# First half of a hybrid attention layer: gate weights split on ACT and DVE instead of POOL, meta columns copied on POOL, squares of x moved into stick-breaking, the first gate pair's weights made ahead

## The chip, the cores and the metric

The kernel runs on 1 core of one Trainium2 chip. Its metric is the time of one execution on the device in microseconds (us), the median of several runs. A core has five engines that run on their own and wait for each other by semaphores: PE (matrix products into PSUM), DVE (vector), ACT (scalar and activation), POOL (general) and SP, which here issues every DMA from one queue in order.

## The reference

One decoder layer, float32, on 2048 tokens of width 1024 with 16 meta tokens ahead of them. All projections come from one matrix `w_in`:

```python
xn = rms_norm(h, norm_gain[l])
proj = xn @ w_in[l]
sb_q, sb_k, sb_v, sw_q, sw_k, sw_v, sb_z, sw_z, g_sb, g_sw = jnp.split(proj, offsets, axis=-1)
o_sb = stick_breaking_attention(sb_q, sb_k, sb_v, valid)          # 8 heads of 64, all earlier keys
o_sw = sliding_window_sink_attention(rope(sw_q), rope(sw_k), sw_v, attn_sinks, valid)   # 16 heads, window 128
y_sb = (o_sb * jax.nn.silu(sb_z)) @ w_branch_sb[l]
y_sw = (o_sw * jax.nn.silu(sw_z)) @ w_branch_swa[l]
merged = jax.nn.sigmoid(g_sb) * y_sb + jax.nn.sigmoid(g_sw) * y_sw
h = h + merged @ w_out[l]
return rms_norm(h, final_norm_gain)[:, BLOCK:]
```

In stick-breaking attention the weight of a key is its sigmoid times the product of (1 - sigmoid) over the keys between it and the query, so it is a running product along the row of scores.

## The kernel before, in words

**Precision.** Every float32 operand is held as two tiles, h (rounded to what PE multiplies) and l (the remainder), and a product is three matmuls: h by h, h by l, l by h. For weights `split` makes the two from a loaded `raw` tile of 128 x 1024. Two switches say where: `hsplit` puts h on ACT (L109) or on POOL (L111), `vsplit` puts l on DVE or on POOL (both L112). Results are evacuated the same way (`evac_split`, L115 on ACT and L116 on DVE). `weights` loads, splits and stores the two halves in DRAM (`kept`), so that the second half of the sequence only loads them.

**Halves and stages.** The sequence (stored in reverse) is worked in two halves of two groups, a group being 512 tokens; a gate or projection tile is 128 columns of `w_in` times a group: 24 matmuls (L415 to L417). Each half has three stages: sliding window (its projections, with that attention between them), stick-breaking, and pairs. Then come the last two gate tiles and the normalised x of the next half, and after both halves the closing stage (`finish`: branch projections, merge, output projection, norm).

**Stick-breaking** (`stick`): 8 heads by 2 groups are 16 units (h, g). A unit's first row loads its keys, values and queries (`load_kv`, `load_q`: kt, vc, q). A row is scores on PE (L1038), a sigmoid on ACT (L1041), a running product on DVE (the scans L1048 and L1050). Where the row ends at the oldest keys, its last 16 columns, the meta tokens, are copied to a small tile (L1054, ACT). Five steps later the row is transposed (L1063), split by ACT and DVE, and multiplied with the values (L1094); meta columns go through `turn_meta` (L1073). `weave` puts these steps between the gate tiles' matmuls: `gts[1]` and `gts[2]` run alone first, `gts[3]` to `gts[REST - 1]` woven in (REST is 12 in the first half, 18 in the second).

**Pairs**: two gates over two groups are a 2 x 2 block product, done in seven products of 12 matmuls each (L685, `seven`) instead of eight. Its x operands, sums of group tiles, are made once on DVE and ACT (`sums_of_x`, L601 to L627); its weight operands t1, t3, t2, t4 by `pair_weights` from two raw tiles a and b (h on ACT, L647; l on DVE, L648; the sums s and s4, L653 to L658). The first three take wh and wl tiles, of which there are three each, shared with all other weights. The first half has six pairs; for the first three of them (`plain`) the two columns' own weights are stored for the second half, for the others the pair's operands. Each result is evacuated through L700 to L715 and gated (sigmoid on ACT, L724; products on DVE, L726 and L730; o is loaded into the ring of four tiles xs, `ring_x`).

**Squares.** The second half's RMS norm needs sums of squares of 1024 tokens: 16 tiles of x, each loaded into the same ring and squared with an accumulator on ACT (L1367), four per pair during the first four pairs.

**Order.** PE's instructions run in the order of the program. DVE, ACT, POOL and SP are ordered by a planner that simulates the kernel when it is built, so an instruction may be moved ahead of others on its engine; on the chip each engine then runs its list in order. Tiles of a name rotate: `tmp` has 7, xs 4, raw 2, wh and wl 3 each; a new use waits until the old one has been read.

Of the kernel before, what the change touches and what calls it, by code (L numbers as in the profile page):

```python
# [47 lines left out]
def tile_kernel(ctx, tc, x, xt, meta, metat, gain, w_in, w_sb, w_sw, w_out, sinks, fgain,  # L48
# [104 lines left out]
    def drain(*gens):  # L153
        for _ in chain(*gens):
            pass
# [194 lines left out]
    def sums():  # L350
        return tp.tile([P, 2, 4], F32, tag="ssq", name="ssq", bufs=3)
# [278 lines left out]

    def pair_weights(bp, ca, cb, plain):

        t1, t3, t2 = ([wp.tile([P, KT, P], F32R, tag=t, name=t, bufs=3) for t in ("wh", "wl")] for _ in range(3))
        t4 = [bp.tile([P, KT // 2, P], F32R, tag=t, name=t, bufs=2) for t in ("s4h", "s4l")]
        key = w_in.name, ca, cb
# [4 lines left out]
        else:  # L640
# [19 lines left out]
            if plain:  # L660
                for c in (ca, cb):
                    kept[w_in.name, c] = [dram(f"{e}_{w_in.name}_{c}", [P, KT, P], F32R) for e in "hl"]
                for k, t in zip(kept[w_in.name, ca], t1):
                    DMA(k, t)
                for k, t, u in zip(kept[w_in.name, cb], t5, t2):
                    DMA(k[:, lo], t)
                    DMA(k[:, hi], u[:, hi])
            else:
                kept[key] = []
                for n, ts in enumerate((t1, t3, t2, t4)):  # L670
                    kept[key].append([dram(f"p{n}{e}_{ca}", list(t.shape), F32R) for e, t in zip("hl", ts)])
                    for k, t in zip(kept[key][n], ts):
                        DMA(k, t)
# [292 lines left out]

    def stick(groups, bp):
        kt, vc = {}, {}
        rows_of = {}
        mask = []  # L970
        bp.tile([P, 4, P], F32R, tag="v", name="vc", bufs=5)
# [46 lines left out]
        def row(h, g, n, j):  # L1018

            if n == j == 0:  # L1020
                load_kv(h, g)
                state[h, g] = {"q": load_q(h, g), "last": {}}
            st = state[h, g]
            last = st["last"]
# [28 lines left out]
            if end:  # L1053
                A.copy(pair(h, g)[0][:, j, h % 2], r[:, w - NM:w])  # L1054

# [238 lines left out]
    for half, groups in enumerate(halves):  # L1294
# [42 lines left out]
        with tc.tile_pool(name=f"sb{half}", bufs=1, side="left") as bp:  # L1337
            vsplit[0] = False
            side = stick(groups, bp)
            drain(tiles_by_tile(gts[1:3], groups))  # L1340
            rest = REST[half]
            cost_sb = 8 * sum(4 * (4 - g) for g in groups) * 1.31 + 8 * 0.75
            ratio = cost_sb / ((rest - 3) * 10.4)
            weave(tiles_by_tile(gts[3:rest], groups), side, ratio)
            drain(side)
        with tc.tile_pool(name=f"pairs{half}", bufs=1, side="left") as bp:
            hsplit[0] = vsplit[0] = True
            ts = [mk() for mk in gts[rest:rest + 2]]
            hsplit[0] = vsplit[0] = False
            sums_q = sums_of_x(bp, groups)  # L1350
# [8 lines left out]
            next(sums_q)  # L1359
            next_sums = {g: sums() for g in halves[1]}  # L1360
            squared = [(g, i, f) for g in halves[1] for i in range(4) for f in range(2)]
            for n in todo:
                if half == 0:
                    for g, i, f in squared[4 * n:4 * n + 4]:
                        t = ring_x()
                        DMA(t, x[g * GT + i * P:g * GT + (i + 1) * P, f * GT:(f + 1) * GT])
                        A.activation(t, t, AF.Square, accum_out=next_sums[g][:, f, i:i + 1])  # L1367
                if half == 0 and n == 4:
# [77 lines left out]
```

## Time and profile before

| | |
|---|---|
| median of 3 runs | 2150.14 us (2148.88 to 2153.46) |
| profiled execution | 2152.05 us, its span 2150.3 us |
| instructions | 29875 |
| DMA | 389.8 MB, mean 181 GB/s |
| sliding window, first half | to about 361 us |
| gts[1], gts[2] alone | 361 to 383 us |
| stick-breaking woven with gates, first half | 383 to 603 us |
| last single gates and pairs, first half | 603 to 770 us |
| stick-breaking and pairs, second half | about 1140 to 1690 us |
| closing stage | from about 1720 us |

How to read the profile: a row of the timeline gives start, duration, engine, source line, operation, the tile written and the tiles read, with the idle time before it and what ended that in brackets. A row of the waits says which instruction waited for which: total us, times, longest. A row of stretches gives, for one stretch of the span, the busy us of PE, PEld (weight loads, beside PE), DVE, ACT and POOL with their counts, the granted PE clock, the mean busy share of the DMA engines and GB/s. SPq rows are DMAs being issued; a long one has stood at the head of the queue.

### The profile page before, as it was taken

To read this page: it belongs to the slowest core of one execution; us is meant where nothing else is said; L and a number is where in the kernel's file an instruction comes from. 1 tells how busy PE (TensorE), PEld (TensorE's weight loads), DVE (VectorE), ACT (ScalarE), POOL (GpSimd) and SP (SyncE) were. 2 spreads that over 40 slices of the span, in tenths; PEclk is the share of its full clock that TensorE was granted. 3 is DMA by queue.
4 is the path that set the end of the run, shared out by engine and by line. 5 is a ranking of instruction groups with operands and counts; after the bars stand their busy time and mean duration, and the time that the engine had idled before them with its cause. 6 is when DMAs were issued, how large, how long until landed. Compare 5 with 4: busy or idle time off the path is not lost.

```text
span 2150.3 us, 29875 instructions
## 1 busy us (share of the span) xinstructions
PE 2097.5 (98%) x10426; PEld 1740.7 (81%) x10426; DVE 1503.4 (70%) x2360; ACT 1070.5 (50%) x2541; POOL 244.1 (11%) x303
## 2 busy tenths in 40 slices
PE   8999999999987999999999999999999999999998
PEld 7788887877866878888888888888888888887887
DVE  7897884788895753677765888889986436554453
ACT  6677774555643433677663666666652301221121
POOL 2122334111000010022220000000000132000000
PEclk9999999999998999999999999999999999999999
DMA  9855545655436985444447333433226785558432
GB/s 337 303 171 184 190 154 193 207 188 173 138 133 215 360 298 169 155 142 157 148 152 214 95 128 113 128 98 114 94 84 206 264 320 184 201 202 298 152 113 78
DMA packets 178838, 389.82 MB, mean 181 GB/s; under 512 B 23200, under 2 KB 41440, under 8 KB 178688
## 3 DMA queue, kind: packets, MB, share of 16 engines
q1 hardware_dynamic: 178688, 387.92, 53.1%
q8 instruction: 82, 1.34, 0.3%
q14 instruction: 68, 0.56, 0.1%
HBM read 242.07 MB, written 145.70 MB: 180 GB/s over the span
## 4 chain that ended last, share of the span: by engine, by line
PE 63%; DVE 3%; ACT 1%; issue 1%; DMA 0%; DVEq 0%; SPq 0%; ACTq 0%
PE ps_g L415 7%; PE ps_g L416 7%; PE ps_g L417 7%; PE ps_o L1094 4%; PE ps_z L1038 4%; PE ps_t L1063 4%; PE ps_z L685 2%; PE ps_t L685 1%; PE ps_g L237 1%; PE ps_g L238 1%; PE ps_g L236 1%; PE ps_z L238 1%; PE ps_z L237 1%; PE ps_z L236 1%; PE ps_z L885 1%; PE ps_t L238 1%
## 5 line engine op out<-in xcount | busy, mean ns | idle before, releaser
L415 PE MATMUL ps_g<-xh,wh 128*128 128x512 f32 x1224 | 502.7, 411 | 8.8 <-ACT xh L1146 6.7
L416 PE MATMUL ps_g<-xl,wh 128*128 128x512 f32 x1224 | 481.4, 393 | 0.3 <-DVE xl L390 0.2
L417 PE MATMUL ps_g<-xh,wl 128*128 128x512 f32 x1224 | 480.9, 393 | 0.0
L417 PEld LDWEIGHTS ps_g<-xh,wl 128*128 128x128 f32 x1224 | 230.6, 188 | 51.5
L415 PEld LDWEIGHTS ps_g<-xh,wh 128*128 128x128 f32 x1224 | 231.7, 189 | 46.1 <-ACT xh L1146 6.7
L416 PEld LDWEIGHTS ps_g<-xl,wh 128*128 128x128 f32 x1224 | 231.9, 189 | 36.7 <-DVE xl L1147 1.3
L1041 ACT ACTIVATE row<-ps_z 128x512 f32<-128x512 f32 (+2 forms) x320 | 164.9, 516 | 133.0 <-PE ps_z L1038 131.3
L1050 DVE TENSOR_TENSOR_SCAN row<-row 128x528 f32<-128x528 f32 (+1 forms) x192 | 214.7, 1118 | 21.1 <-ACT row L1041 17.5
L1048 DVE TENSOR_TENSOR_SCAN row<-row,mask 128x512 f32<-128x512 f32 (+4 forms) x128 | 149.6, 1173 | 83.3 <-ACT row L1041 82.2
L116 DVE SCALAR_TENSOR_TENSOR wtl<-ps_t,wth 128x512 fp32r<-128x512 f32 (+1 forms) x320 | 189.5, 592 | 18.0 <-ACT wth L115 17.1
L115 ACT ACTIVATE wth<-ps_t 128x512 fp32r<-128x512 f32 (+1 forms) x320 | 170.3, 532 | 46.5 <-PE ps_t L1063 44.6
L1038 PE MATMUL ps_z<-kt,q 128*128 128x512 f32 (+4 forms) x640 | 178.8, 354 | 0.3 <-ACT row L1041 0.3
L1063 PE MATMUL ps_t<-ident,row 128*128 128x128 f32 x1088 | 172.0, 273 | 6.7 <-DVE wtl L116 6.1
L1063 PEld LDWEIGHTS ps_t<-ident,row 128*128 128x128 f32 x1088 | 134.3, 140 | 41.7 <-DVE wtl L116 9.1
L111 POOL TENSOR_SCALAR wh<-raw 128x1024 fp32r<-128x1024 f32 (+1 forms) x49 | 52.2, 1065 | 994.0 <-PE ps_o L685 545.1
L1038 PEld LDWEIGHTS ps_z<-kt,q 128*128 128x128 f32 x640 | 117.4, 188 | 22.1 <-ACT row L1041 0.8
L1094 PE MATMUL ps_o<-wth,vc 128*128 128x512 f32 (+1 forms) x320 | 130.9, 409 | 2.4 <-DMA q<-qd 1.3
L893 ACT ACTIVATE sc<-sc,nm 128x129 f32<-128x129 f32 x256 | 100.0, 393 | 40.9 <-DVE nm L891 40.1
L1094 PE MATMUL ps_o<-wtl,vc 128*128 128x512 f32 (+1 forms) x320 | 117.1, 366 | 0.1
L275 ACT CAST ringl<-gt 128x512 fp32r<-128x512 f32 x32 | 19.9, 622 | 162.3 <-DVE gt L273 161.4
L583 ACT ACTIVATE tmp<-ps_g 128x512 f32<-128x512 f32 x72 | 43.0, 598 | 76.0 <-PE ps_g L417 63.5
L885 PEld LDWEIGHTS ps_z<-kk,q 128*128 128x128 f32 x512 | 69.7, 190 | 6.6 <-DVE q L866 0.7
(419 smaller groups left out, 4161.5 us busy)
## 6 DMA issues: line engine op xcount, KB each, us to landing
wh<-h_in_w_in SPq DMA_DIRECT2D x60, 512.0 KB
wl<-l_in_w_in SPq DMA_DIRECT2D x60, 512.0 KB
raw<-in_w_in SPq DMA_DIRECT2D x50, 512.0 KB
h_in_w_in<-wh SPq DMA_DIRECT2D x41, 512.0 KB
l_in_w_in<-wl SPq DMA_DIRECT2D x41, 512.0 KB
q<-qd SPq DMA_DIRECT2D x128, 128.0 KB
vc<-vd SPq DMA_DIRECT2D x48, 256.0 KB
kd<-tmp SPq DMA_DIRECT2D x32, 256.0 KB
```

Source lines behind the costliest of these rows:

```text
L115: A.activation(h, acc, AF.Copy, scale=scale)
L116: V.scalar_tensor_tensor(l, acc, scale, f32(h), op0=ALU.mult, op1=ALU.subtract)
L415: T.matmul(acc, lhsT=wh[:, k, :], rhs=xh[g][:, k, :], start=k == 0, stop=False)
L416: T.matmul(acc, lhsT=wh[:, k, :], rhs=xl[g][:, k, :], start=False, stop=False)
L417: T.matmul(acc, lhsT=wl[:, k, :], rhs=xh[g][:, k, :], start=False, stop=k == KT - 1)
L893: A.activation(sc[:, hh, :], sc[:, hh, :], AF.Exp, bias=nm[:, hh:hh + 1], accum_out=den[:, hh:hh + 1])
L1038: T.matmul(acc[:, :b - a], lhsT=lq, rhs=kt[h][:, k0 + a:k0 + b], start=t == 0, stop=t == 1)
L1041: A.activation(r[:, a:b], acc[:, :b - a], AF.Sigmoid, scale=-1.0)
L1048: V.tensor_tensor_scan(r[:, :w], r[:, :w], mask[0][:, :w], 1.0, op0=ALU.mult, op1=ALU.max)
L1050: V.tensor_tensor_scan(r[:, :w], r[:, :w], r[:, :w], last[j], op0=ALU.mult, op1=ALU.min)
L1063: T.transpose(tr[:, j * P:(j + 1) * P], rows_of[h, g, n - (j > i), j][:, k0:k0 + P], ident)
L1094: T.matmul(o[:, :n], lhsT=v, rhs=r, start=first and r is wh, stop=last and r is wl)
```

## The change

Five edits. In both halves the switches are set to ACT and DVE from the stick-breaking stage on, and no longer back; so the first half's gate weights (gts[1] to gts[11], the last two gates) and, in `finish`, those of both branch projections are split there and not on POOL. The copy of the 16 meta columns moves from ACT to POOL. The squares of the second half's x move from the pairs into the first half's stick-breaking: from the third unit on, each unit loads two tiles into a ring of four of their own (xq), and squares the two that the unit before it loaded. The weights of the first half's first pair are made between gts[1] and gts[2], with t4 in `tmp` tiles, and stored, both as the columns' own weights and as the pair's operands; in the pairs they are loaded. `hsplit` is not switched off before the pairs.

```diff
-    def pair_weights(bp, ca, cb, plain):
+    def pair_weights(bp, ca, cb, plain, early=False):
...
-        t4 = [bp.tile([P, KT // 2, P], F32R, tag=t, name=t, bufs=2) for t in ("s4h", "s4l")]
+        if early:
+            t4 = [tmp(F32R).rearrange("p (k c) -> p k c", k=KT // 2) for _ in range(2)]
+        else:
+            t4 = [bp.tile([P, KT // 2, P], F32R, tag=t, name=t, bufs=2) for t in ("s4h", "s4l")]
...
-            else:
+            if early or not plain:
                 kept[key] = []
...
-    def stick(groups, bp):
+    def stick(groups, bp, squared=()):
...
                 state[h, g] = {"q": load_q(h, g), "last": {}}
+                n1 = len(state) - 1
+                for t, acc in xq:
+                    A.activation(t, t, AF.Square, accum_out=acc)
+                del xq[:]
+                if n1 > 1:
+                    for src, acc in squared[2 * n1 - 4:2 * n1 - 2]:
+                        t = bp.tile([P, GT], F32, tag="xq", name="xq", bufs=4)
+                        DMA(t, src)
+                        xq.append((t, acc))
...
             if end:
-                A.copy(pair(h, g)[0][:, j, h % 2], r[:, w - NM:w])
+                G.tensor_copy(pair(h, g)[0][:, j, h % 2], r[:, w - NM:w])
...
-            vsplit[0] = False
-            side = stick(groups, bp)
-            drain(tiles_by_tile(gts[1:3], groups))
+            hsplit[0] = vsplit[0] = True
+            next_sums = {g: sums() for g in halves[1]} if half == 0 else {}
+            side = stick(groups, bp, [(x[g * GT + i * P:g * GT + (i + 1) * P, f * GT:(f + 1) * GT], ssq[:, f, i:i + 1])
+                                      for g, ssq in next_sums.items() for i in range(4) for f in range(2)])
+            drain(tiles_by_tile(gts[1:2], groups))
             rest = REST[half]
+            if half == 0:
+                pair_weights(None, gss[0][rest + 2][0], gss[0][rest + 3][0], True, True)
+            drain(tiles_by_tile(gts[2:3], groups))
...
-            hsplit[0] = vsplit[0] = True
             ts = [mk() for mk in gts[rest:rest + 2]]
-            hsplit[0] = vsplit[0] = False
...
-            next_sums = {g: sums() for g in halves[1]}
-            squared = [(g, i, f) for g in halves[1] for i in range(4) for f in range(2)]
             for n in todo:
-                if half == 0:
-                    for g, i, f in squared[4 * n:4 * n + 4]:
-                        t = ring_x()
-                        DMA(t, x[g * GT + i * P:g * GT + (i + 1) * P, f * GT:(f + 1) * GT])
-                        A.activation(t, t, AF.Square, accum_out=next_sums[g][:, f, i:i + 1])
```

More of the change, by code (lines that the diff above doesn't have):

```diff
@@ L964, in window @@
         return sw_k, sw_v, sw_q, attend, ending
-    def stick(groups, bp):
+    def stick(groups, bp, squared=()):
         kt, vc = {}, {}
         rows_of = {}
-        mask = []
+        mask, xq = [], []
         bp.tile([P, 4, P], F32R, tag="v", name="vc", bufs=5)
```

## The prediction

> **What bounds the kernel now.** First the page: busy time by engine.
>
> ```profile
> PE 2097.5 (98%) x10426; PEld 1740.7 (81%) x10426; DVE 1503.4 (70%) x2360; ACT 1070.5 (50%) x2541; POOL 244.1 (11%) x303
> ```
>
> TensorE is the bound: of the 2150.3 us only 53 lie outside its busy time. The change takes no matmul away and PE's order is the program's, so only PE's waits, and the slow pace that follows some of them, can move. Second the stages, as stretches (PE, PEld, DVE, ACT and POOL busy, PE clock, DMA share, GB/s): the end of sliding window, stick-breaking, and the pairs (two rows) of the first half; then stick-breaking and pairs of the second.
>
> ```profile
> 320.00:390.00 70.00, 67.76 (x328) 55.33 (x327) 30.71 (x57) 27.93 (x80) 26.37 (x27) 1.00 0.65 211
> 390.00:603.00 213.00, 205.05 (x1144) 171.22 (x1143) 174.17 (x223) 128.25 (x322) 24.16 (x16) 1.00 0.51 165
> 603.00:690.00 87.00, 68.51 (x279) 54.58 (x278) 67.03 (x102) 33.33 (x60) 1.72 (x3) 0.91 0.50 169
> 690.00:767.00 77.00, 74.36 (x317) 60.60 (x316) 57.13 (x82) 32.01 (x54) 6.89 (x4) 0.97 0.90 332
> 1143.00:1603.00 460.00, 458.86 (x2525) 384.95 (x2524) 402.51 (x490) 279.26 (x598) 0.00 (x0) 1.00 0.36 114
> 1603.00:1690.00 87.00, 85.89 (x378) 70.44 (x377) 53.98 (x83) 22.37 (x38) 3.57 (x2) 1.00 0.60 208
> ```
>
> The second half, which only loads ready weights, loses about 1 us of PE in each stage; the first half loses 8 in stick-breaking and 21 in the pairs. Third, whom PE waits for between 320 and 870 us (total, times, longest).
>
> ```profile
> PE ps_z L685 <- ACT wh L647: 10.0, 2, 7.8
> PE ps_z L685 <- DVE tmp L700: 5.7, 1, 5.7
> PE ps_t L1063 <- DVE wtl L116: 5.3, 6, 1.5
> PE ps_z L685 <- DVE wl L648: 2.8, 2, 2.2
> PE ps_t L685 <- DVE tmp L709: 2.6, 1, 2.6
> PE ps_o L1094 <- DMA q<-qd: 1.3, 1, 1.3
> PE ps_zm L533 <- DVE vt L116: 1.0, 1, 1.0
> PE ps_zm L533 <- DVE tmp L526: 0.9, 1, 0.9
> PE ps_o L1094 <- ACT tmp L1098: 0.8, 1, 0.8
> ```
>
> L685 is the pairs, the L1063, L1094 and L533 rows are stick-breaking and its run-up. These rows are what can be won.
>
> **The pairs stage and its whole loss.** PE's matmuls in order of time:
>
> ```profile
> 603.11 0.39 PE L415 MATMUL ps_g<-xh,wh 128*128 128x512 f32 x1
> 625.13 0.39 PE L685 MATMUL ps_g<-xl,wh 128*128 128x512 f32 x1
> 625.35 0.39 PE L685 MATMUL ps_g<-xh,wl 128*128 128x512 f32 x1
> 646.27 0.63 PE L685 MATMUL ps_z<-t3l,wh 128*128 128x512 f32 x1
> 646.70 0.63 PE L685 MATMUL ps_z<-t3h,wl 128*128 128x512 f32 x1
> 770.00 0.60 PE L373 MATMUL ps_t<-ident,rs 128*128 128x128 f32 x4
> ```
>
> Two gates over two groups are 4 x 24 matmuls, six pairs 6 x 84. These 600, at the undisturbed step of about 0.227 us (625.13 to 625.35), make 136.1 us; the stage takes 770.0 - 603.1 = 166.9. So 30.8 are lost: 21.1 of waits (10.0 + 5.7 + 2.8 + 2.6) and 9.7 mostly of matmuls that, after a wait, start 0.43 us apart (646.27 to 646.70). What makes the waits shows on SP's queue, ACT and DVE:
>
> ```profile
> 645.42 11.11 SPq L58 DMA_DIRECT2D xs<-in_x  x4
> 678.23 0.63 ACT L1367 ACTIVATE xs<-xs 128x512 f32<-128x512 f32 x1 [8.99 <-issue]
> 688.15 1.03 ACT L647 CAST wh<-s 128x1024 fp32r<-128x1024 f32 x1
> 663.95 0.46 SPq L58 DMA_DIRECT2D raw<-in_w_in  x1
> 670.26 0.69 DVE L653 TENSOR_TENSOR s<-raw 128x512 f32<-128x512 f32 x1 [4.17 <-DMA raw<-in_w_in]
> ```
>
> The loads of x for the squares take slots of the ring of four (xs) that also holds the gates' o. Four of them stand 11.11 us at the head of SP's only queue; behind them wait the gate stores, which free tmp tiles, and the next raw weights. ACT works in order and sits 8.99 us before a square, so the third pair's wh is cast only at 688.15: PE's 7.8 us wait. The second pair's 2.8 (2.2 + 0.6) follow the first block in the same way.
>
> **Squares moved.** 16 loads of 256 KB and 16 x 0.63 = 10.1 us of ACT leave this stage. What is late next there is DVE's own work.
>
> **First pair's weights made sooner.** Here 8 loads (6 of 512, 2 of 256 KB) replace 7.8 us of DVE (3 x 1.23 + 6 x 0.69, rows at 574 and 581 below) and some 4 of ACT. t2's tile comes free last, at about 625; with 6.3 us for a load (663.95 to 670.26) it is there at 631.3, and PE, without its first wait of 2.2, reads it at 633. The second half does exactly this, and has one wait left:
>
> ```profile
> 1637.73 0.50 PE L685 MATMUL ps_z<-t3h,wh 128*128 128x512 f32 x1 [1.00 <-DVE tmp L700]
> ```
>
> In the first half the second pair's splits share DVE meanwhile, so this wait lies between 1.0 and the 5.7 of now.
>
> **The last two gates' weights** also leave POOL; two of its subtractions lie on the chain of the 2.6 us wait on L709. I leave a residue of 6 us in the stage (3 at L700 with slow steps, 3 for the rest): the gain is 30.8 - 6 = 24.8; its ends are 28.5 (the second half's 1.0, and a us of slow steps) and 18 (L700 as now with its slow steps, and 5 more).
>
> **Stick-breaking: gate weights off POOL.** What POOL's subtraction does to DVE, and how a split on ACT and DVE went in the same stage:
>
> ```profile
> 403.90 2.39 POOL L112 TENSOR_TENSOR wl<-raw,wh 128x1024 fp32r<-128x1024 f32 x1
> 404.14 3.27 DVE L1048 TENSOR_TENSOR_SCAN row<-row,mask 128x528 f32<-128x528 f32 x1 [1.14 <-ACT row L1041]
> 432.70 1.26 DVE L1048 TENSOR_TENSOR_SCAN row<-row,mask 128x528 f32<-128x528 f32 x1
> 574.02 1.23 DVE L112 TENSOR_TENSOR wl<-raw,wh 128x1024 fp32r<-128x1024 f32 x1 [0.86 <-ACT wh L109]
> 550.00:575.00 25.00, 25.00 (x143) 21.33 (x142) 21.38 (x29) 17.72 (x43) 0.00 (x0) 1.00 0.35 123
> ```
>
> The same scan took 1.26 us alone and 3.27 beside the subtraction: DVE stood for 2.0 us and PE waited soon after. On DVE the subtraction takes 1.23 (and the cast on ACT 1.03), so DVE's load falls by 0.8 a split, and in the stretch that ends with such a split PE had no wait (25.00 of 25). Two of the six L1063 waits come instead from making the first pair at the stage's end:
>
> ```profile
> 581.11 0.69 DVE L653 TENSOR_TENSOR s<-raw 128x512 f32<-128x512 f32 x1 [1.34 <-DMA raw<-in_w_in]
> 600.71 0.66 PE L1063 MATMUL ps_t<-ident,row 128*128 128x128 f32 x4 [1.48 <-DVE wtl L116]
> ```
>
> So all of 5.3 + 1.3 + 1.0 + 0.9 + 0.8 = 9.3 us is open; ends 9.3 and 4, and I take 9.3, since the rows without POOL show no wait. New in this stage are the squares: two per head and group, loaded one unit (213 us / 16, some 13) ahead into four tiles of their own, 10.1 us more on ACT, whose 128 of 213 have room, while 64 meta copies leave it. Should a load be late, ACT stands as DVE did at 581 (1.34 us). Eight such bursts cost 0 (as the split at 574) to 10; I take 3.
>
> **The early pair's own price.** It puts 2 loads, the 6 stores of before (2 MB) and 8 new ones (3.5 MB) at some 345 to 385 us, on SP ahead of the stage's kt, q and vc loads.
>
> ```profile
> DMA  0004295096451899800028998999999999999910
> 360.18 0.60 ACT L583 ACTIVATE tmp<-ps_g 128x512 f32<-128x512 f32 x1 [1.30 <-PE ps_g L417]
> 372.03 0.60 ACT L583 ACTIVATE tmp<-ps_g 128x512 f32<-128x512 f32 x1 [4.84 <-PE ps_g L417]
> ```
>
> ACT idles 4.84 of each 5.4 us there, and DVE's 30.71 of 70 lie before and after, so the arithmetic is covered; without that cover it would cost its 7.8. The DMA engines (slices of 2 us from 320) idle from 354 to 360 but are full from 362 to 396. And the pair takes all three wh tiles: gts[2] needs t1's tile back, after its stores, and a's raw tile. That waits for t5 (tmp tiles that gate stores of about 361 free) and four DVE steps, so until 365; a load of 6.3 and a split of 2.3 make 373.8, and PE, done with gts[1] (372.03), wants it at 371.8. The low end is 2; were s4 queued behind t2, whose tile is free at 372, 11. In the first pair of before the sums s went ahead of the tiles that waited for room, so I take 4.
>
> **Other edits cost nothing.** The meta copies go to a POOL that is nearly idle and are read five steps later. In the closing stage 16 splits now also fall to ACT and DVE; even where DVE is fullest, and POOL was subtracting beside it, PE did not wait:
>
> ```profile
> 1800.00:1825.00 25.00, 25.00 (x112) 20.71 (x111) 23.88 (x31) 7.69 (x13) 9.18 (x9) 1.00 0.74 234
> ```
>
> If that cover failed, the eight half-size splits would cost at most their own 8 x 0.69 = 5.5.
>
> **Sum.** 24.8 + 9.3 - 3 - 4 = 27.1 us off the profiled execution's 2152.05, 2125. That run is 1.9 above the median of the runs shown, so 2123 against the median; I say 2124.
>
> **Rivals.** (a) The squares' stall moves with them: ACT idled up to 8.99 us before a square, and in stick-breaking every row and every transpose passes through ACT. Without my 3 the gain is 30.1; at 30.1 / 16 = 1.9 us a square all is lost, and from 2.2 on the kernel is slower. At 3.5 (one in four waits 8.99 and the others 1.7) it is 56: 2124 - 3 + 56 = 2177. Against it: own tiles, and a whole unit of lead. 6%. (b) The early pair starves gts[2], gts[3] and the first rows: 14 us (11 and 3 more) in place of 4, 2134. For it the full DMA slices, against it the idle ones before. 14%. (c) DVE still bounds the pairs' first 45 us and L700 is as late as now: residue 12 in place of 6, 2130. For it, DVE busy 67 of 87. 12%. (d) The copies on POOL hold up DVE's scans, as its subtractions did.
>
> ```profile
> L878 POOL COPY sc<-skb x64: 185/190/1187, 48.5 to 1101.2; 128x4 f32<-128x4 f32 x64
> ```
>
> Small copies on POOL took 0.19 us (median) and up to 1.19. 128 x 0.19 = 24 us; six subtractions held DVE for 12 and left PE some 5 (5.3 + 1.3 + 0.8 less 2.3 of the first pair), so 24 make 10: 2134. Against it, 0.19 is a sixth of a scan. 5%. The Trainium skill, "SBUF — State Buffer", section "Who interferes with whom", says that a VectorE instruction with two SBUF inputs contends with a GpSimd one that reads SBUF, and that the later of the two blocks fully. The 3.27 us scan agrees; by this rule each copy that starts first would hold a scan, 2134, and the sum without it stays 2124. (e) The waits only change places and nothing is gained: 2150, 3%.
>
> **The numbers.** The forecast has 60%, with 2114 to 2133; up to 2141 the range takes in (b), (c) and (d), and leaves out (a), (e) and a tail. 0.2% (4.3 us) is about what a measurement of this kernel tells from none. Faster: nearly all of the forecast, (b), (c) and (d), 0.88; same 0.05; slower 0.07.
>
> **What would show it.** Right: no xs load at SP's head near 645; no wait on L647 in the pairs; no scan of 3 us beside POOL; over 80 us of PE in the 87 after stick-breaking. Wrong: a new PE wait at 372 or 383 on L109, L112 or kt; ACT idle before squares in stick-breaking; L700 waited for over 5 us.

## The result and the profile after

The changed kernel takes 2139.88 us (median of 4 runs, 2139.07 to 2142.02); the kernel before, on the same chip, 2151.8 (2148.88 to 2153.47). The ratio is 0.9948, 95% interval 0.993 to 0.9965: 11 to 12 us faster, where 27 were forecast. The profiled execution takes 2139.68 us, its span is 2138.0, that is 12.3 less than the span before.

Line numbers have moved: before's L647 is now L650, L685 L688, L700 L703, L1038 L1050, L1041 L1053, the scans L1048 and L1050 L1060 and L1062, L1054 L1066, L1063 L1075, L1094 L1106; the squares are L1028. First the page, then the same stretches as in the prediction, with one more around the last single gates of the first half.

```profile
PE 2091.8 (98%) x10426; PEld 1736.9 (81%) x10426; DVE 1497.1 (70%) x2389; ACT 1079.3 (50%) x2442; POOL 184.1 (9%) x373
```

```profile
320.00:390.00 70.00, 56.58 (x260) 44.85 (x259) 33.56 (x64) 29.10 (x74) 10.51 (x17) 0.90 0.60 209
390.00:603.00 213.00, 207.35 (x1143) 173.75 (x1142) 165.00 (x221) 133.19 (x295) 15.56 (x61) 1.00 0.64 210
603.00:690.00 87.00, 80.50 (x358) 64.56 (x358) 72.20 (x112) 34.27 (x58) 4.85 (x9) 0.98 0.55 182
690.00:767.00 77.00, 77.00 (x343) 63.74 (x342) 57.20 (x87) 29.24 (x40) 0.56 (x4) 1.00 0.94 343
780.00:830.00 50.00, 50.00 (x224) 41.38 (x224) 23.05 (x35) 18.45 (x31) 0.00 (x0) 1.00 0.72 236
1143.00:1603.00 460.00, 458.72 (x2524) 384.54 (x2523) 412.48 (x510) 273.03 (x535) 12.68 (x64) 1.00 0.34 109
```

PE's busy time rose by 2.3 us in stick-breaking and by 12.0 in the 87 us after it, and the last pairs run without a gap (77.00 of 77). But the first stretch, 320 to 390, has 11.2 us less of PE than before, and its clock fell to 0.90. The waits of PE between 320 and 870 us say where:

```profile
PE ps_g L415 <- ACT wh L109: 12.3, 1, 12.3
PE ps_z L688 <- DVE tmp L703: 3.5, 1, 3.5
PE ps_t L1075 <- DVE wtl L116: 3.0, 4, 1.5
PE ps_t L1075 <- DVE wm L116: 2.0, 3, 1.6
PE ps_z L688 <- DVE wl L651: 1.3, 2, 0.7
PE ps_z L688 <- ACT wh L650: 1.0, 2, 0.5
```

One wait, on the weights of `gts[2]`, is as long as all the others together (12.3 us against 12.8, with three small ones that are left out above); the 10.0, 5.7, 2.8 and 2.6 us of the pairs have become 1.0, 3.5, 1.3 and none. Below are the rows of ACT, DVE, SP's queue and PE that lead to the long one, in order of time.

```profile
371.56 0.60 ACT L583 ACTIVATE tmp<-ps_g 128x512 f32<-128x512 f32 x1 [4.84 <-PE ps_g L417]
372.06 0.61 ACT L650 CAST tmp<-raw 128x512 fp32r<-128x512 f32 x1
372.70 0.69 DVE L651 TENSOR_TENSOR tmp<-raw,tmp 128x512 fp32r<-128x512 f32 x1 [10.58 <-ACT tmp L650]
373.42 0.69 DVE L657 TENSOR_TENSOR raw<-raw 128x512 f32<-128x512 f32 x1
374.15 0.69 DVE L658 TENSOR_TENSOR s<-raw 128x512 f32<-128x512 f32 x1
374.88 0.69 DVE L661 TENSOR_TENSOR tmp<-raw,s 128x512 f32<-128x512 f32 x1
376.77 0.55 SPq L58 DMA_DIRECT2D raw<-in_w_in  x1
382.70 1.04 ACT L109 CAST wh<-raw 128x1024 fp32r<-128x1024 f32 x1 [5.31 <-DMA raw<-in_w_in]
383.79 0.80 PE L415 MATMUL ps_g<-xh,wh 128*128 128x512 f32 x1 [12.27 <-ACT wh L109]
386.07 0.63 PE L416 MATMUL ps_g<-xl,wh 128*128 128x512 f32 x1
386.50 0.63 PE L417 MATMUL ps_g<-xh,wl 128*128 128x512 f32 x1
```

Read it backwards. PE waited for the cast of `gts[2]`'s raw tile (382.70), which waited 5.31 us for its load (issued at 376.77); the load waited for the raw tile of a, which s4 (L661, 374.88) is the last to read; s4 stood behind three steps of DVE, and the first of them, t5's remainder at 372.70, behind t5's cast, which stood in ACT's list behind the second sigmoid of `gts[1]` (371.56). DVE idled 10.58 us before it. After the wait PE's matmuls came 0.43 us apart (386.07 to 386.50) until about 389.9, and then 0.23.

To follow the parts through the runs I use four stretches of the profiled execution, cut at events that every kernel has: the last product of the first half's stick-breaking (L1094 before, L1106 after), the first product of the transposed sums after the pairs (L373, at 770.00 before), the last product of the second half's stick-breaking, and the end. In us:

| kernel | first stick-breaking ends | the same, from `ch<-ph` | pairs | to the end of the second | rest | span |
|---|---|---|---|---|---|---|
| before | 602.78 | 278.09 | 167.22 | 833.57 | 546.73 | 2150.3 |
| after | 615.48 | 290.79 | 145.27 | 829.30 | 547.95 | 2138.0 |
| squares alone (e4) | 607.52 | 281.94 | 152.20 | 829.17 | 549.61 | 2138.5 |
| switches alone (e5) | 596.73 | 271.64 | 162.14 | 834.22 | 546.81 | 2139.9 |
| no early pair (e1) | 602.67 | 276.58 | 152.17 | 829.30 | 547.36 | 2131.5 |

After against before: +12.7, -21.95, -4.3, +1.2, together -12.3.

How far can such numbers be trusted? Every kernel here has the same lists on ACT, DVE and POOL for the first 324 us, and still their last common row on POOL, which writes `ch`, comes anywhere from 324.09 us (e11) to 326.88 (e14). The first row is of before, the second of e14:

```profile
324.69 0.64 POOL L918 TENSOR_SCALAR_AFFINE_SELECT ch<-ph 128x512 fp32r<-128x512 f32 x1 [1.92 <-ACT tmp L558]
326.88 0.64 POOL L918 TENSOR_SCALAR_AFFINE_SELECT ch<-ph 128x512 fp32r<-128x512 f32 x1 [1.93 <-ACT tmp L558]
```

So the end of the first stick-breaking differs by up to 2.8 us between executions before any edit can act. e14 left this stage as it was and ended it at 604.78, 2.0 us later than before, and 2.2 were there at this row. The third column therefore counts from `ch<-ph`; further down, "counted" means this. Each number is still of one execution.

### The profile page after: what moved, and what is told of

Its sections match the earlier page's. It is cut to its first block, busy times and chain, and to the rows that moved or that the text cites. A ratio compares the mean times of both kernels' runs of the same rounds, so it can differ in the third digit from the quotient of the medians.

```text
span 2138.0 us, 29936 instructions
## 1 busy us (share of the span) xinstructions
PE 2091.8 (98%) x10426; PEld 1736.9 (81%) x10426; DVE 1497.1 (70%) x2389; ACT 1079.3 (50%) x2442; POOL 184.1 (9%) x373
## 4 chain that ended last, share of the span: by engine, by line
PE 82%; DVE 8%; DMA 5%; ACT 3%; issue 2%; SPq 1%; DVEq 0%; ACTq 0%
PE ps_g L415 11%; PE ps_g L417 11%; PE ps_g L416 11%; PE ps_o L1106 5%; PE ps_t L1075 5%; PE ps_z L1050 5%; PE ps_o L934 3%; PE ps_z L888 2%; PE ps_z L688 2%; PE ps_t L688 2%; PE ps_g L688 2%; PE ps_g L237 1%; PE ps_g L238 1%; PE ps_g L236 1%; PE ps_z L238 1%
## 5 line engine op out<-in xcount | busy, mean ns | idle before, releaser
L415 PE MATMUL ps_g<-xh,wh 128*128 128x512 f32 x1224 | 503.2, 411 | 19.1 <-ACT wh L109 12.3
L415 PEld LDWEIGHTS ps_g<-xh,wh 128*128 128x128 f32 x1224 | 231.8, 189 | 56.1 <-ACT wh L109 12.7
L1053 ACT ACTIVATE row<-ps_z 128x512 f32<-128x512 f32 (+2 forms) x320 | 165.4, 518 | 180.0 <-PE ps_z L1050 176.5
L1062 DVE TENSOR_TENSOR_SCAN row<-row 128x528 f32<-128x528 f32 (+1 forms) x192 | 210.6, 1097 | 19.8 <-ACT row L1053 15.4
L1060 DVE TENSOR_TENSOR_SCAN row<-row,mask 128x512 f32<-128x512 f32 (+4 forms) x128 | 144.2, 1131 | 69.1 <-ACT row L1053 68.0
L1050 PE MATMUL ps_z<-kt,q 128*128 128x512 f32 (+4 forms) x640 | 178.9, 355 | 0.0
L1075 PE MATMUL ps_t<-ident,row 128*128 128x128 f32 x1088 | 171.9, 273 | 6.3 <-DVE wtl L116 3.8
L1075 PEld LDWEIGHTS ps_t<-ident,row 128*128 128x128 f32 x1088 | 134.4, 140 | 41.1 <-DVE wtl L116 6.7
L1050 PEld LDWEIGHTS ps_z<-kt,q 128*128 128x128 f32 x640 | 117.4, 188 | 22.1 <-ACT row L1053 0.4
L1106 PE MATMUL ps_o<-wth,vc 128*128 128x512 f32 (+1 forms) x320 | 130.7, 409 | 1.0 <-ACT tmp L1110 0.9
L1106 PE MATMUL ps_o<-wtl,vc 128*128 128x512 f32 (+1 forms) x320 | 117.1, 366 | 0.2
L112 DVE TENSOR_TENSOR wl<-raw,wh 128x1024 fp32r<-128x1024 f32 (+1 forms) x51 | 58.4, 1145 | 45.6 <-ACT wh L109 40.8
L1066 POOL COPY xs<-row 128x16 f32<-128x16 f32 x128 | 28.8, 225 | 668.8 <-DVE row L1062 590.1
L301 ACT ACTIVATE sq<-res 128x512 bf16<-128x512 f32 x32 | 20.2, 632 | 109.3 <-DVE res L297 107.0
```

The source lines that it names most:

```text
L415: T.matmul(acc, lhsT=wh[:, k, :], rhs=xh[g][:, k, :], start=k == 0, stop=False)
L1050: T.matmul(acc[:, :b - a], lhsT=lq, rhs=kt[h][:, k0 + a:k0 + b], start=t == 0, stop=t == 1)
L1053: A.activation(r[:, a:b], acc[:, :b - a], AF.Sigmoid, scale=-1.0)
L1060: V.tensor_tensor_scan(r[:, :w], r[:, :w], mask[0][:, :w], 1.0, op0=ALU.mult, op1=ALU.max)
L1062: V.tensor_tensor_scan(r[:, :w], r[:, :w], r[:, :w], last[j], op0=ALU.mult, op1=ALU.min)
L1075: T.transpose(tr[:, j * P:(j + 1) * P], rows_of[h, g, n - (j > i), j][:, k0:k0 + P], ident)
```

## The experiments

**Which part costs and which wins.** Three runs do one part alone or leave one out.

```diff
 # e1: after, without the early pair
-            if half == 0:
-                pair_weights(None, gss[0][rest + 2][0], gss[0][rest + 3][0], True, True)
 # e4: before, with the squares in stick-breaking as in the change
 # e5: before, with hsplit = vsplit = True from stick-breaking on, never switched back
```

> The changed kernel without its early pair: the first pair's weights are made in the pairs stage as before, the other edits stay. Theory A (the early pair's cost is PE's wait for gts[2]): the 12.3 us wait at 384 us and the slow matmuls after it (some 2 us) go, the pairs stage loses again the first pair's own waits (2.2 and some more at L700, 4 to 6 in all with slow steps), and the two waits at the end of stick-breaking stay: 2139.9 - 14.3 + 5, about 2131. Rival B (the early pair is worth what it costs, and the wait at 384 is only where PE stands for a stage that other work bounds): the time stays at 2138 to 2142, with new waits for kt, q or rows in stick-breaking.

Measured 2133.56 us (2132.15 to 2134.05), ratio 0.9922 (0.9908 to 0.9937): theory A. The wait at 383.79 is gone, stick-breaking ends 12.8 us sooner than in after (14.2 counted), and the pairs are 6.9 longer, with the waits at their start that the first pair made there had before (2.23 us on its wl, 5.61 on L703). So the early pair loses 12.8 to win 6.9: without it the kernel is some 6 us faster. The longest of PE's waits that are left in this stage, 1.94 of 7.4 us, stands at its start:

```profile
386.57 0.63 ACT L1028 ACTIVATE xq<-xq 128x512 f32<-128x512 f32 x1 [2.45 <-DMA h_in_w_in<-wh]
387.20 0.36 ACT L1053 ACTIVATE row<-ps_z 128x256 f32<-128x256 f32 x1
387.62 0.82 PE L1050 MATMUL ps_z<-kt,q 128*128 128x272 f32 x2 [1.94 <-ACT row L1053]
```

ACT sat 2.45 us before the first square (the bracket names only the last event before it; what the square waited for is not shown), the row's sigmoid stood behind it, and PE's next scores behind that: 1.94 us, and again matmuls at the slow step.

> The kernel before with one edit alone: squares by own tiles in stick-breaking. My reading of the pairs stage (the squares' loads block SP's queue and ACT): the waits at 661 and 689 (2.8 and 7.8 us with some 3 us of slow matmuls) go or fall under 1 us each, and stick-breaking pays 3 us for squares that wait for their loads: 2151.8 - 13.5 + 3, about 2141. Rival (DVE bounds the pairs, SP's block only hides in it): the waits stay above 6 us in all, 2148 to 2155.

Measured 2139.68 us (2138.73 to 2142.27), ratio 0.9954 (0.9937 to 0.9971). In the pairs the squares' move wins 15.0 us, and 4.4 more behind them: the stretch of 780 to 830 us, which had a gap on L388 of 1.84 us and a clock of 0.97 before, is full. In stick-breaking it costs 4.7 (3.9 counted). The rows of before for that gap, a row of the timeline and one of the stretches:

```profile
799.60 0.51 PE L415 MATMUL ps_g<-xh,wh 128*128 128x512 f32 x1 [1.84 <-ACT xh L388]
```

```profile
780.00:830.00 50.00, 47.94 (x205) 38.82 (x204) 22.98 (x35) 15.68 (x28) 0.00 (x0) 0.97 0.72 241
```

> The kernel before with one part of the change: from the first half's stick-breaking on, the gate weights are split on ACT and DVE and no longer on POOL. Meta columns stay on ACT, the squares stay in the pairs, no early pair. Theory S (the POOL splits were what rows and matmuls of the first stick-breaking waited for, and this part stands by itself): the stage's last meta product ends at about 597 to 599 us instead of 602.1, PE's waits behind POOL (about 5 us there) are gone, the pairs keep their 168 us with the waits at the squares, time 2144 to 2147. Theory N (the switch only moves the split onto ACT and DVE, whose rows then come later, and what the change won in this stage came with the POOL copies): stage ends at 601 to 604, time 2148 to 2152.

Measured 2142.63 us (2141.41 to 2147.12), ratio 0.9967 (0.9957 to 0.9976): theory S for the stage, and some 1.4 us better than its time, since the pairs won too. Stick-breaking ends 6.05 us sooner (6.45 counted), with the splits that held DVE gone; the longest of PE's waits in it were:

```profile
PE ps_t L1063 <- DVE wtl L116: 3.1, 2, 1.7
PE ps_o L1094 <- ACT tmp L1098: 1.2, 3, 0.8
```

The 3.1 us are two waits at 579.81 and 594.66, where the raw tiles of a coming pair hold DVE up, as two did before. In the pairs the wait on L709 at 765 is gone too, which with the slow matmuls after it gives most of that stage's 5.1; e4 has it gone as well, so these two wins don't add.

**The early pair's 12.8 us: what are they?** First the third gate's weights, made ahead of the pair and so out of its reach.

```diff
 # e2: after, with
+            gt2 = [mk() for mk in gts[2:3]] if half == 0 else None
             if half == 0:
                 pair_weights(None, gss[0][rest + 2][0], gss[0][rest + 3][0], True, True)
-            drain(tiles_by_tile(gts[2:3], groups))
+            drain(tiles_by_tile([lambda: gt2[0]] if half == 0 else gts[2:3], groups))
```

> The changed kernel with one order changed: gts[2]'s weights are asked for before the early pair's, so they take the earlier raw and wh tiles and the pair takes the next. Theory A (gts[2] starves because its raw tile is a's, held until s4): the wait at 372 to 384 goes; gts[3], which now follows in a's raw tile, is wanted at 382.4 and can be ready at about 385: a wait of 1 to 4 us in its place. 2139.9 - 14.3 + 3, about 2128. Rival B (DMA: the 5.5 MB of stores and the stage's loads fill the engines, whoever comes first): a wait of 8 us or more stays, at gts[3] or the first rows, and the time is over 2135.

Measured 2142.34 us (2140.3 to 2145.64), ratio 0.9965 (0.9952 to 0.9978). The wait on L109 fell from 12.27 to 1.23 us as expected of the chain, and the stage ended at 615.02 all the same. Theory A's 2128 failed; the time is rival B's, with a wait of 6.3 us where it named 8:

```profile
382.93 0.50 PE L415 MATMUL ps_g<-xh,wh 128*128 128x512 f32 x1 [1.23 <-ACT wh L109]
395.30 1.21 PE L1050 MATMUL ps_z<-kt,q 128*128 128x512 f32 x2 [6.31 <-DMA kt<-kd]
```

Now the first rows wait for their keys. PE's busy time shows that the loss is only moved: of the 80 us from 360 to 440 it is busy for 66.4 in after, 65.4 in e2, and 75.1 in e1, the measure. The first stretches of 20 us, in this order:

```profile
360.00:380.00 20.00, 11.52 (x51) 9.12 (x49) 6.56 (x9) 5.08 (x8) 0.90 (x3) 0.91 0.67 200
380.00:400.00 20.00, 16.17 (x60) 12.74 (x61) 2.45 (x2) 4.60 (x9) 0.00 (x0) 0.75 1.03 368
```

```profile
360.00:380.00 20.00, 20.00 (x90) 16.55 (x89) 7.56 (x10) 5.63 (x9) 0.83 (x2) 1.00 0.85 291
380.00:400.00 20.00, 11.94 (x45) 8.66 (x44) 6.25 (x7) 4.61 (x9) 1.83 (x4) 0.83 1.02 342
400.00:420.00 20.00, 16.86 (x94) 13.86 (x93) 14.63 (x20) 15.66 (x40) 2.10 (x5) 1.00 1.03 379
```

```profile
360.00:380.00 20.00, 20.00 (x90) 16.41 (x89) 3.19 (x4) 4.69 (x7) 1.26 (x3) 1.00 0.79 249
380.00:400.00 20.00, 18.06 (x85) 15.03 (x84) 11.02 (x13) 10.30 (x26) 1.83 (x4) 0.91 0.96 329
```

Then the pair's scratch tiles. In the change t5 and s4 take `tmp` tiles; here they come from the ring of the squares, which is empty at that time.

```diff
 # e3: after, in pair_weights, called with the pool bp
+            own = (lambda dt=F32: bp.tile([P, GT], dt, tag="xq", name="own", bufs=4)) if early else tmp
-            s4 = tmp().rearrange("p (k c) -> p k c", k=KT // 2)
+            s4 = own().rearrange("p (k c) -> p k c", k=KT // 2)
-                t5 = [tmp(F32R).rearrange("p (k c) -> p k c", k=KT // 2) for _ in range(2)]
+                t5 = [own(F32R).rearrange("p (k c) -> p k c", k=KT // 2) for _ in range(2)]
```

> The changed kernel with t5 and s4 of the early pair in three of the xq tiles and not in tmp tiles; orders, transfers and bytes as they are. Theory A1 (what is late is t5's cast, which was queued behind gts[1]'s second sigmoid for a tmp tile, and with it s4 and a's raw tile): t5 is cast at about 361, s4 done by 366, raw for gts[2] lands by 373, PE waits 2 to 4 us in place of 12.3: about 2130. Rival B (the transfers are late, not the tile): raw is asked for some 9 us earlier but lands only after 378, and PE waits 8 us or more: over 2135. Rival C (t1's wh tile, held by its stores, is what gts[2] waits for): the wait stays at 12: 2139 to 2142.

Measured 2136.13 us (2134.94 to 2136.46), ratio 0.9935 (0.992 to 0.9949). t5's cast now comes at 366.69 and not at 372.06, and the wait falls:

```profile
366.69 0.62 ACT L651 CAST own<-raw 128x512 fp32r<-128x512 f32 x1 [4.31 <-DMA ow<-os]
376.31 1.04 ACT L109 CAST wh<-raw 128x1024 fp32r<-128x1024 f32 x1 [2.50 <-DMA raw<-in_w_in]
377.41 0.80 PE L415 MATMUL ps_g<-xh,wh 128*128 128x512 f32 x1 [4.74 <-ACT wh L109]
```

The stage ends at 608.49: the tiles are worth 7.0 of the 12.8 (8.1 of 14.2 counted). More of the wait stayed than theory A1 said (4.74 us for 2 to 4), and the time is 6 us above its 2130. By its bracket the cast now waited 4.31 us for the stores of the sliding window's results. (Line numbers of e3 and e16 are one above those of after, those of e10 and e17 two.) Two runs leave out the early pair's eight stores of 3.5 MB.

```diff
 # e9: e2, and e16: e3, each with
-            if early or not plain:
+            if not plain:
```

> The run with the third gate's weights made before the early pair (2142.3, where the loss showed as 6.3 us of PE waiting for kt's load at 395 us), and now without the early pair's eight stores of 3.5 MB: the early pair is computed and thrown away, and made again in the pairs stage. Theory T (the pair's stores and loads fill the queues in front of kt and q): the wait for kt falls below 1.5 us, first stick-breaking ends at 602 to 606 instead of 614.3, the pairs take about 153 us, time 2133.5 to 2138. Rival O (it is the pair's work on ACT and DVE, or its two raw loads, that hold up the first rows): waits of 6 us or more remain there, stage end over 610, time over 2143.

Measured 2138.25 us (2135.79 to 2142.22), ratio 0.9944 (0.9926 to 0.9962). The wait for kt is gone, the stage ends at 609.25: between the two theories, 5.8 us better than e2, 6.6 worse than without an early pair (6.6 and 6.8 counted; the profiled execution is the slowest of the five, 4 us above their median). At 384.77 PE waits 2.21 us for `gts[3]`'s wh (its load is late), and in the next rows 1.59, 1.24, 1.63 and 2.20.

> The changed kernel with the early pair where the change put it, its scratch tiles from the squares' ring, and its eight stores of 3.5 MB left out (the pair is made again in the pairs stage). The early pair costs the first stick-breaking 12.8 us (end 615.5 against 602.7). Own tiles alone gave back 7.0 (608.5), leaving out the stores alone 5.8 (609.25, with the third gate first). Theory A (the two are separate causes and add up: tiles that DVE's rows and the pair's parts wait for, and stores ahead of kt and q): stage end 602 to 605, time 2133 to 2136. Rival S (they are the same delay, or what is left is the pair's work on ACT and DVE and its raw loads): stage end 606.5 to 609.5, time 2137 to 2141.

Measured 2140.43 us (2138.56 to 2141.03), ratio 0.9958 (0.9943 to 0.9973); the stage ends at 607.79. Rival S: with own tiles the stores cost nothing that shows (without them the stage ends 0.7 us sooner, and is 0.8 longer counted), not another 5.8. The wait that stays can be followed to the ring of two raw tiles:

```profile
368.04 0.69 DVE L662 TENSOR_TENSOR own<-raw,s 128x512 f32<-128x512 f32 x1
369.34 0.62 SPq L58 DMA_DIRECT2D raw<-in_w_in  x1
375.42 1.04 ACT L109 CAST wh<-raw 128x1024 fp32r<-128x1024 f32 x1 [3.09 <-DMA raw<-in_w_in]
376.52 0.80 PE L415 MATMUL ps_g<-xh,wh 128*128 128x512 f32 x1 [5.33 <-ACT wh L109]
```

The pair holds both raw tiles until s4; PE goes on 7.2 us after the next load's issue. In e1 that load was issued at 363.46.

**The same work in another place.** If the place is the fault, the pair should be cheap later in the stage.

```diff
 # e10: e3, with the call moved from ahead of gts[2] to ahead of gts[7]; e17: ahead of gts[9]
-            weave(tiles_by_tile(gts[3:rest], groups), side, ratio)
+            def mid(mk):
+                if half == 0:
+                    pair_weights(bp, gss[0][rest + 2][0], gss[0][rest + 3][0], True, True)
+                return mk()
+            weave(tiles_by_tile([*gts[3:LATE], lambda: mid(gts[LATE]), *gts[LATE + 1:rest]], groups), side, ratio)
```

> The changed kernel with the early pair's six scratch tiles from the ring of the squares (2136.1) and the early pair moved from ahead of the third gate to between the seventh and the eighth, in the middle of the stick-breaking. Theory P (the early pair costs 12.8 us by its place: there the engines are still starting the first rows, q and kt are being loaded, and gates 2 and 3 have no finished weights): stage end 601 to 605, pairs 146 us, time 2126 to 2131, faster than without an early pair. Rival C (the pair's 19 us of work on ACT and DVE together, its loads and 5.5 MB of stores cost as much wherever they stand in this stage): stage end 608 or later, time 2134 or more.

Measured 2130.64 us (2129.61 to 2131.77), ratio 0.9911 (0.9892 to 0.9929): theory P. With the same tiles, loads, stores and steps the pair cost 5.8 us at its old place (e3) and costs 2.6 here (stage end 605.31), 6.1 and 2.4 counted; pairs 147.0.

> The kernel with the early pair between the seventh and eighth gate (2130.6, stage end 605.3, against 602.7 without an early pair), the pair now between the ninth and tenth gate, some 50 us later, when squares and the first loads of q and kt are over. Theory P (what is left of the pair's price, 2.6 us, is its meeting with the squares and their loads between 420 and 460 us): PE's waits at 449.8 and 462.6 (1.67 and 0.54) go and none of that size comes between 480 and 560, stage end 603 to 604, time 2128 to 2130. Rival C (the pair costs 2 to 3 us wherever it stands after the first rows): stage end 605 to 606.5, time 2130 to 2132. Rival D (its parts, stores and the reload at the pairs' start now come too late): the first pair waits for its tiles, time over 2132.

Measured 2128.68 us (2125.34 to 2130.03, 5 runs), ratio 0.9895 (0.9876 to 0.9914). The stage ends at 603.95, 1.3 later than without an early pair (1.2 counted), the waits of 1.67 and 0.54 us are gone, and 0.59 and 0.40 came at 514 and 535; pairs 145.3. The direction is theory P's; the step from e10 is smaller than the 2.8 us that executions differ by, and the intervals overlap. This is the fastest kernel of the study, 11 us below the changed one.

**The squares' 4.7 us.** Three runs put them later in the stage, two keep them in the pairs with loads asked for a pair ahead.

```diff
 # e7: e1, squares in the rows' ring: 15 buffers for both, instead of 12 and 4
-                        t = bp.tile([P, GT], F32, tag="xq", name="xq", bufs=4)
+                        t = bp.tile([P, RW], F32, tag="row", name="xq", bufs=15 if squared else 12)[:, :GT]
 # e11: e1, squares four units later (its expectation says five); e12: the same on e10
-                if n1 > 1:
-                    for src, acc in squared[2 * n1 - 4:2 * n1 - 2]:
+                if n1 > 5:
+                    for src, acc in squared[2 * n1 - 12:2 * n1 - 10]:
 # e14: before, a pair's four loads one pair ahead; e15: the same on e10
+                    for t, acc in xq:
+                        A.activation(t, t, AF.Square, accum_out=acc)
+                    xq = load_x(n + 1)
```

> The changed kernel without the early pair (2133.6) and with the squares' tiles drawn from the ring of the rows (15 buffers for both instead of 12 and 4), so that a square can't run before the row three quarters of a ring back is done. Its list of ACT spreads the 16 squares over some 75 rows instead of about 35. Theory H (the squares cost 4.8 us of the stage because all 16 with their loads run between 399 and 444 us, when q and kt of the first heads are still being loaded): PE's waits between 425 and 441 fall from about 2.8 us to under 1, the stage ends at 597 to 600 instead of 602.0, time 2129 to 2132. Rival W (it is the squares' own ACT time, 16 of about 0.65 us, wherever they run): end 601 to 603, time 2133 to 2135. Rival R (the rows need their 12 buffers): waits of PE on rows grow, time over 2135.

Measured 2135.77 us (2132.74 to 2139.89), ratio 0.9936 (0.9913 to 0.9958), stage end 608.38: rival R, PE's waits from 370 to 612 us grew from 7.4 to 13.3 (the profiled execution is the slowest of the four, 4 us above their median). The squares did spread, from 403 to 503 us, but since rows and squares now share buffers this says nothing of theory H.

> The changed kernel without the early pair (2133.6), the squares asked for five blocks of rows later (blocks 6 to 14 instead of 1 to 9, buffers as in the change). In ACT's list the 16 now stand among rows 9 to 38 and none among the first eight rows. Theory H (the squares cost 4.7 us because they and their loads stand among the first rows, where ACT waits for a square's load and the row behind it, and PE, waits too): PE's waits between 385 and 445 us fall from about 4.2 us to under 2, the first stick-breaking ends at 598 to 600.5 instead of 602.7, time 2129 to 2132. Rival W (a square costs its ACT time wherever it stands in this stage): end 602 to 604, time 2133 to 2135.

Measured 2134.25 us (2132.2 to 2134.56), ratio 0.9932 (0.9915 to 0.9948), stage end 601.67. The wait at 387 is gone, but 1.30 and 3.17 us came at 398 and 423, where ACT stood 4.09 and then 3.68 us before squares whose loads were late. Theory H fails: the stage is 1.0 us shorter by its end and 1.0 longer counted. But the squares hardly moved in time, from 386.6 to 425.5 us in e1 to 395.6 to 427.3 here; what they cost when spread over the whole stage, with buffers of their own, stays open.

> Both: the early pair in the middle of the stick-breaking with its scratch tiles from the squares' ring (2130.6, stage end 605.3), and the squares five blocks later. If the two add: stage end 601 to 603.5, pairs 146, time 2126 to 2129. Rival K (squares, the pair and its 5.5 MB of stores now stand in the same 60 us and share one ring of four tiles): stage end 605 to 609, time 2130 to 2134.

Measured 2136.78 us (2134.07 to 2138.35), ratio 0.9945 (0.993 to 0.996), stage end 609.50: rival K, and somewhat worse than it said.

> The kernel before, where the squares stay in the pairs and keep their tiles, but a pair's four loads are asked for one pair ahead, so that a square doesn't stand in ACT's list behind a load just issued. Nothing else of the change. Theory L (what cost 15 us in the pairs and 4.4 us after them was ACT standing still for the squares' late loads, not the squares' place): first stick-breaking ends at 602.8 as before, the pairs take 152 to 157 us instead of 167.2, time 2131 to 2137. Rival M (the ring of four tiles, shared with the sums of x, or ACT's 16 squares themselves hold the pairs up; moving them out was needed): pairs 162 or more, time 2143 or more.

Measured 2148.46 us (2147.05 to 2151.44), ratio 0.9996 (0.9987 to 1.0005): nothing gained, rival M. The loads, asked for sooner, stood at the head of SP's queue as before, because their tiles come from the ring that the gates' o also use:

```profile
647.55 10.85 SPq L58 DMA_DIRECT2D xs<-in_x  x4
679.55 0.63 ACT L1375 ACTIVATE xs<-xs 128x512 f32<-128x512 f32 x1 [8.56 <-issue]
691.72 0.80 PE L685 MATMUL ps_z<-t2h,wh 128*128 128x512 f32 x1 [8.49 <-ACT wh L647]
```

Compare 11.11, 8.99 and 7.8 before. The move gave the squares another place and tiles of their own at once; whether such tiles would have done in the pairs was not run. Behind the pairs, up to the end of the second stick-breaking, this run took 829.2 us like e4, and PE has no gap from 780 to 830 (50.00 of 50), with the squares still in the pairs. So the 4.4 us that e4 won there don't need the move. And since this run's median is that of before all the same, one profile does not show what they are worth.

> The kernel with the late early-pair (2130.6: stick-breaking ends at 605.3, pairs 147.0) with its squares taken out of the stick-breaking and made in the pairs with loads one pair ahead. By theory L the stick-breaking gives back the squares' 4 to 6 us (end 599 to 601.5) and the pairs grow by at most 3: time 2125 to 2129. By rival M the pairs grow by 10 or more: time 2134 or more.

Measured 2134.46 us (2133.04 to 2137.79), ratio 0.9936 (0.992 to 0.9953). Stick-breaking gave back 6.9 us (598.42; 5.1 counted) and the pairs took them (153.93): neither theory's numbers, and no better than e10.

**The copies.**

> The kernel with the late pair (2130.6), its meta columns copied on ACT again. Switches alone ended the first stick-breaking 6.05 us sooner and squares alone 4.74 us later, which would make 601.5; with both and the copies on POOL it ended at 602.7. Theory G (the POOL copies cost that 1.2 us, because a copy waits for DVE's row and holds the row's tile or a port): stage end about 604 instead of 605.3, and a little in the second half's stick-breaking, time 2128.5 to 2130. Rival A (the copies on POOL win, because ACT with the squares and the splits has no room for 32 copies more): end 606 to 608, time 2131.5 to 2134. Rival 0: nothing, within 1 us of 2130.6.

Its edit on e10 is `A.copy` in place of `G.tensor_copy` for the meta columns. Measured 2130.51 us (2128.42 to 2132.24), ratio 0.9917 (0.9902 to 0.9932), stage end 605.15: rival 0 (counted the stage is 1.2 us longer than e10's, of which the time shows nothing).

## Why the prediction was right or wrong

The sum went 24.8 + 9.3 - 3 - 4 + 0 = 27.1. By the table it was 21.95 + 6.45 - 4.9 - 14.2 + 3.05, which makes the span's 12.3 (6.45, 4.9 and 14.2 are counted from `ch<-ph`: e5 against before, e1 against e5, after against e1; the 4.9 is what squares and copies take).

*The early pair, -4, is the step that failed.* The prediction had the place (a wait at 372 to 384 on L109 is its own sign of being wrong) and the chain: t1's tile, a's raw tile, t5, four DVE steps, one load, one split. It let t5 start when `tmp` tiles came free, some 361 us, and set its high end, 11, by s4 behind t2. But t5's cast stood in ACT's list behind a sigmoid that waits for PE until 371.56, and s4 behind it: a wait of 12.27 us, above the high end, with slow matmuls after it, and 14.2 in the stage. "ACT idles 4.84 of each 5.4 us, so the arithmetic is covered" was true of the engine and useless for the chain: an idle engine that works in order does nothing for an instruction behind one that waits. Rival (b) had this, 14 us at 14%; it named starved rows too, which came only in e2. Its own 2134 failed since the other three terms were short as well.

*The squares in stick-breaking, -3.* 4.7 alone, 5.9 between e5 and e1 (3.9 and 4.9 counted); inside the ends of 0 to 10, and rival (a)'s mechanism at a small price: ACT stood up to 2.45 us before a square with a row behind it. The lead of one unit did not hold: all 16 squares ran between 387 and 426 in e1, since the planner moved them ahead, into the busiest time of the DMA engines (share 0.95 to 0.96).

*Gate weights off POOL, 9.3.* 6.05 (6.45 counted), inside the ends of 9.3 and 4. The error is in "two of the six L1063 waits come from making the first pair at the stage's end" and so go with it: they come from raw tiles, and the second pair's raws, now loaded at that time, bring them back (1.46 and 0.55 us in after, 1.36 and 0.56 in e10).

*The pairs, 24.8.* 21.95, within 18 to 28.5; the signs came nearly as named: two waits on L650 of 0.5 us each where none was named, the x loads gone from SP's head, 80.5 and 77 us of PE. L703 stayed at 3.5 us, between the 1.0 and 5.7 named; the residue is 9, not 6. Half of rival (c) is in it.

*Other edits, 0.* The 4.3 us won between the pairs and the second half were not looked for: the gap at 799.60 was in the trace, outside the stretch that was quoted (and by e14 they don't need the squares' move). Some 1.2 us were lost in the rest of the kernel; in other runs this stretch lost up to 4.4 (e3, 551.2 against 546.73), and its cause was not traced.

*Rival (d), copies on POOL.* Wrong, and the scans say so directly (groups by line, first half's stick-breaking: min, median and longest in ns): before, with POOL's splits, the longest scan over the mask took 3315; after, with copies and no splits on POOL, 1260 (the other scans went from 2864 to 1319), and it is the copy that was held, up to 1116.

```profile
L1048 DVE TENSOR_TENSOR_SCAN row<-row,mask x64: 426/1224/3315, 384.8 to 584.2; 128x512 f32<-128x512 f32 x32, 128x528 f32<-128x528 f32 x8, 128x400 f32<-128x400 f32 x8, 128x272 f32<-128x272 f32 x8
```

```profile
L1066 POOL COPY xs<-row x64: 197/198/1116, 401.9 to 608.0; 128x16 f32<-128x16 f32 x64
```

```profile
L1060 DVE TENSOR_TENSOR_SCAN row<-row,mask x64: 425/1222/1260, 400.6 to 598.0; 128x512 f32<-128x512 f32 x32, 128x528 f32<-128x528 f32 x8, 128x400 f32<-128x400 f32 x8, 128x272 f32<-128x272 f32 x8
```

The Trainium skill, "SBUF — State Buffer", section "Who interferes with whom", says that the one that comes second waits for the whole instruction of the other. The rows agree: a POOL subtraction of 2.4 us held scans for 2, and beside copies of 0.2 us no scan was held by anything of that size. Rival (d) took from the rule that there is a wait and not how long it can be.

## What to carry to other kernels

Work that is moved ahead costs what its chain of tiles and lists costs at the new place, not what its engines have idle there: follow each scratch tile to what frees it, and each instruction to what stands before it in its engine's list. The same preparation cost 12.8 us at the start of a stage, 5.8 there with scratch tiles of its own, and with these 1.3 to 2.6 further on in the stage (14.2, 6.1 and 1.2 to 2.4 counted); so try two places before giving up such a move. When one delay is removed and the stage ends as late as before, look for the next one in the same 20 us: tiles, raw buffers and the queue in front of the keys each held up the same start, and their prices did not add. And before a difference of 2 us between two profiles is explained, look whether it was there before the first edited instruction.

## What was not expected of the hardware

The slow step can follow a wait of 2 us and stay away after one of 3. After 12.27 us of waiting PE's matmuls came 0.43 us apart for about 6 us. After the 1.94 us at 387.62 in e1 they did so too, and the granted clock of those 20 us was 0.91 (row of 380 to 400 above):

```profile
388.24 0.63 PE L415 MATMUL ps_g<-xh,wh 128*128 128x512 f32 x1
388.67 0.63 PE L416 MATMUL ps_g<-xl,wh 128*128 128x512 f32 x1
```

But after 3.17 us in e11 the matmuls came 0.23 us apart at once:

```profile
423.11 0.50 PE L1106 MATMUL ps_o<-wth,vc 128*128 128x512 f32 x1 [3.17 <-ACT tmp L1110]
424.16 0.40 PE L415 MATMUL ps_g<-xh,wh 128*128 128x512 f32 x1
424.39 0.39 PE L416 MATMUL ps_g<-xl,wh 128*128 128x512 f32 x1
```

So the length of a wait alone doesn't tell whether slow matmuls follow it; what does is not shown here.
